# Block sums of the second feed-forward product by accumulating DMAs, its seven products in another order, and small tiles padded

## The chip, the cores and the metric

The kernel runs on 1 core of one Trainium2 chip. The metric is device time in microseconds; 3 runs of the kernel before gave 877.93, 878.17 and 878.65, median 878.17. The profile is of one further execution.

## The reference, cut to what matters

One layer of a streaming encoder on 512 frames of 1024 channels, float32 throughout. Three gated branches (gated linear attention, forgetting attention, attention to 256 memory tokens) are merged and projected, then a feed-forward part follows and a last norm.

```
u = rmsnorm(h) * g_mix
proj = u @ w_in                     # queries, keys, values, gates of three branches
merged = sig(g0)*(o_gla @ w_gla_o) + sig(g1)*(o_fox @ w_fox_o) + sig(g2)*(o_mem @ w_mem_o)
h = h + merged @ w_out
u2 = rmsnorm(h) * g_ffn
h = h + square(relu(u2 @ w_ff1)) @ w_ff2     # 512x1024 @ 1024x4096, then 512x4096 @ 4096x1024
out = rmsnorm(h) * g_final
```

The change concerns the product with `w_ff2` and, by its padding, where some tiles of the branches lie.

## The kernel before

Every large product is done in three TensorE (PE) matmuls: both operands are split into a high part (a cast on ScalarE, ACT) and a low part (a subtraction on VectorE, DVE), and high by high, low by high and high by low are added up in PSUM (`mm3`, lines 118 to 121). Weights come in blocks of 128x1024, 512 KB each, loaded on the SP queue. `split_w` and `split` (lines 111, 112, 171, 172) split them. The hi and lo buffers are three deep (pool `wp`); in the last stage every fourth block uses a buffer of its own, one deep (`bhi`, `blo`, in `split_b`).

The last stage runs over four quarters q of the 4096 hidden channels. A quarter first makes eight 128x512 tiles of the hidden layer, transposed: 24 matmuls with a block of `w_ff1` each, then `act_evac` squares and splits them. Two such tiles make a pair p; of its four 128x256 parts a11, a21 (first tile) and a12, a22 (second) seven forms are kept, in the slots of tiles `ch` and `cl` (high and low): slot 0 as soon as the first tile is there, slots 1 and 2 with the second (a 128x512 split from `sq`), slots 3 to 6 from four differences `ss` (line 888) and a 128x1024 split of them, which is the last to be done.

Then `second(q)` multiplies by the quarter of `w_ff2`, in Strassen's manner (Winograd's form): seven products of half-size blocks in place of eight. Product n takes one slot of the activations and one block of weights. The weights of a quarter are eight tiles `raw`: blocks 11, 12, 22, 21 (stored with the signs that the method needs), each for i = 0 and 1 (pairs 0, 1 and pairs 2, 3). `factor(n, i)` makes the block that product n needs: plain for 1, 2 and 3, and otherwise by adding another block in place on VectorE (`add`, line 906). 5 is block 11 plus 12, 6 is that plus 22, 4 is that plus 21, and 7 is block 12 plus 22. So block 11 is added to three times, each time after the split before has read it. Each step of a product (one i) is 12 matmuls: two row blocks t, two pairs, three matmuls each. The products 1 and 5 stay in PSUM (pool `pa`, tag `a`) over all quarters; 6 and 7 are summed in `R6` and `R7`; 4, 3 and 2 are added to the residual `hN` as they come (`C(i, j, t)` is a 128x512 half of one row block). In the last quarter `evac` combines everything and calls `finish` for each half row: sum of squares on ScalarE, multiplication by the final gain, and behind the second half the row's rsqrt (`ms` on VectorE, `rr` on GpSimd, the POOL engine), two scalings and two stores. The very last product takes both steps i together (`end`).

The order of TensorE is the order in which the program is written. All other engines and the SP queue are ordered by a scheduler when the program is built, so a moved line can move instructions there too. POOL does the merge's additions in the branch stage; between the last of them and the final rsqrts it has only the four rsqrts of the middle norm.

The tiles lie in SBUF pool by pool. A pool on the right side of SBUF holds `acc` and the split branch outputs `ogh`, `ogl` and `omh`, `oml`. They are streamed through TensorE as the moving operand by `branch` (lines 119 to 121 again). In the kernel as built they start 480 bytes past a multiple of 512; `Pm`, `ph` and `pl` of the memory attention start 224 bytes past one; the other large tiles, such as `uhi`, `ofh`, `mh`, `ch`, start 32 past one.

Of the kernel before, what the change touches and what calls it, by code (L numbers as in the profile page):

```python
# [9 lines left out]
F32 = mybir.dt.float32  # L10
# [7 lines left out]
P = 128  # L18
# [14 lines left out]
def chunk_list():  # L33

    L = []
    L += [("T", "w_mem_kv", P * j) for j in range(4)]
    L += [("N", "w_mem_kv", 2 * j, 512) for j in range(4)]
    L += [("G",)]
    L += [("T", "w_in", OFF["fq"]), ("T", "w_in", OFF["fk"])]
    L += [("N", "w_in", 2 * j, OFF["fv"]) for j in range(4)]  # L40
    for j in range(1, 4):
        L += [("T", "w_in", OFF["fq"] + P * j), ("T", "w_in", OFF["fk"] + P * j)]
    for n, c in (("gk", 2), ("gq", 2)):
        L += [("T", "w_in", OFF[n] + P * j) for j in range(c)]
    L += [("N", "w_in", 2 * j, OFF["gv"]) for j in range(4)]
    for n, c in (("gg", 4), ("mq", 4)):
        L += [("T", "w_in", OFF[n] + P * j) for j in range(c)]
    for g, o in (("gate_fox", "w_fox_o"), ("gate_mem", "w_mem_o"), ("gate_gla", "w_gla_o")):
        for j in range(KT):
            L.append(("T", "w_in", OFF[g] + P * j))  # L50
            if j % 2 == 0:
                L.append(("O", o, j // 2))
    for c in range(2):
        L += [("N", "w_out", 2 * j, 512 * c) for j in range(4)]
    for q in range(4):
        L += [("T", "w_ff1", P * (8 * q + j)) for j in range(8)]
        L += [("B", q, i, b) for b in ("11", "12", "22", "21") for i in range(2)]
    return L


# [1 line left out]
def hybrid_block(ctx, tc, chunks, wst, xT, memT, xN, cols, gffn, gfin, wup, cst, out):  # L62
# [6 lines left out]
    def nm(s):  # L69
        uid[0] += 1  # L70
        return f"{s}_{uid[0]}"
# [7 lines left out]
    def pool(name, side=None, bufs=1):  # L79
        return tc.tile_pool(name=name, bufs=bufs, side=side, reuse_waits="tile")  # L80
# [17 lines left out]
    ident, ones, tri, tri64 = (cst_s[:, i * P:(i + 1) * P] for i in range(4))  # L98
    mhalf = cst_s[:, 6 * P:6 * P + 8]
    gmix, gmem, ghead = cols_s[:, 0:8], cols_s[:, 8:16], cols_s[:, 16:20]  # L100

    def load_w(key, eng=None):
        i = index[key]
# [426 lines left out]


    mst = ExitStack()
    mp = mst.enter_context(pool("merge", side="right"))
    acc = [mp.tile([P, S], F32, name=f"acc{j}") for j in range(KT)]

# [37 lines left out]
    with pool("mematt") as ap:  # L573
# [9 lines left out]
        def mem_scores(h):  # L583
            qh, ql = st["q", h]
            mx = ap.tile([P, NT], F32, tag="mx", name=nm("mx"), bufs=2)
            rs = ap.tile([P, NT], F32, tag="rs", name=nm("rs"), bufs=2)
            ri = ap.tile([P, NT], F32, tag="ri", name=nm("ri"), bufs=2)
            Pm = st["p", h] = ap.tile([P, NT, M], F32, tag="Pm", name=nm("Pm"), bufs=2)
            for g in range(2):
                ps = at_([P, 2, M])  # L590
# [42 lines left out]
    with pool("gla") as lp:  # L633
# [13 lines left out]
        def decays(j):  # L647
# [2 lines left out]
                nc.tensor.matmul(pb[:, t * P:(t + 1) * P], la[:, t, j * P:(j + 1) * P], tri64, start=True, stop=True)  # L650
            ep = lp.tile([P, S], F32, tag="ep", name=nm("ep"))
            en = lp.tile([P, S], F32, tag="en", name=nm("en"))
            bl = lp.tile([P, NC, 1], F32, tag="bl", name=nm("bl"))
            dec = lp.tile([P, NC], F32, tag="dec", name=nm("dec"))
            ek = lp.tile([P, NC, 64], F32, tag="ek", name=nm("ek"))
            pb3 = pb.rearrange("p (c t) -> p c t", c=NC)
            nc.vector.tensor_copy(bl, pb3[:, :, 63:64])
# [102 lines left out]

    hp = ctx.enter_context(pool("h"))
    hN = [hp.tile([P, D], F32, name=f"h{t}") for t in range(NT)]
    hss = hp.tile([P, LINE], F32, name="hss")[:, :2 * NT].rearrange("p (t c) -> p t c", c=2)
    gf = hp.tile([P, D], F32, tag="gf", name="gf")
    nc.sync.dma_start(gf, gffn)

# [86 lines left out]
    with pool("ff") as yp:  # L853
# [8 lines left out]
        def split_b(raw):  # L862
            split_n[0] += 1
            own = split_n[0] % 4 == 0
            hi, lo = ((yp if own else wp).tile([P, 1024], F32R, tag=g, name=nm(g), bufs=1 if own else 3)
                      for g in (("bhi", "blo") if own else ("hi", "lo")))
            split(hi, lo, raw)
            return [t.rearrange("p (k c) -> p k c", k=2) for t in (hi, lo)]
# [36 lines left out]
        def add(to, x, op=ALU.add):  # L905
            nc.vector.tensor_tensor(to, to, x, op=op)  # L906

        def evac(q, n, t, ps):
# [24 lines left out]
            if n == 3:  # L933
                add(C(0, 1, t), ps)
                if last:
                    finish(t, 1, 0)
            if n == 2:
                add(C(0, 0, t), ps)
                if last:
                    finish(t, 0, 1)  # L940

        def second(q):
            raw = {(b, i): yp.tile([P, 1024], F32, tag=f"b{b}{i}", name=nm("raw")) for b in ("11", "12", "22", "21")
                   for i in range(2)}
            for (b, i), t in raw.items():
                nc.sync.dma_start(t, wst[index["B", q, i, b]])

            def factor(n, i):

                b11, b12, b22, b21 = (raw[b, i] for b in ("11", "12", "22", "21"))  # L950
                to, x = {1: (b11, None), 5: (b11, b12), 6: (b11, b22), 7: (b12, b22), 4: (b11, b21), 3: (b22, None),
                         2: (b21, None)}[n]
                if x is not None:
                    add(to, x)
                return split_b(to)

            for n, slot in ((1, 0), (5, 3), (6, 4), (7, 5), (4, 2), (3, 6), (2, 1)):
                keep = n in (1, 5)
                if not keep:
                    ps = [mmt() for _ in range(2)]  # L960
                else:
                    ps = held.setdefault(n, [at_() for _ in range(2)] if q == 0 else None)
                end = q == NQ - 1 and n == 2
                steps = [[0, 1]] if end else [[0], [1]]
                for js in steps:
                    w = {i: factor(n, i) for i in js}
# [107 lines left out]
```

## Time and profile before

| | |
|---|---|
| median of 3 runs | 878.17 us (877.93 to 878.65) |
| profiled execution | 879.23 us, span 877.5 us |
| mean granted TensorE clock | 0.988 |
| ScalarE busy in the span | 405.3 us, 46% |
| DMA | 87.75 MB, mean 100 GB/s |
| last stage, four quarters | from about 532 us to the end |

In lines of the timeline the columns are start, duration (both us), engine, line, operation, tiles written and read, shape, count, and in brackets how long the engine sat idle and what ended that. Matmuls overlap: their duration is longer than the distance of their starts, and the distance is what counts for the time. In lines of waits the columns are the total in us, how often, and the longest. In lines of one tile the three numbers are the shortest, median and longest duration in ns. Names in the profile are those of the program without buffer numbers: `a` and `mm` are PSUM tiles, `raw` a loaded block.

### The profile page before, as it was taken

The numbers are of one execution on the slowest core, as the hardware profiler recorded it, in microseconds if no ns is written. First come the engines' busy times: TensorE is split into PE (matmuls) and PEld (weight loads), VectorE is DVE, ScalarE is ACT, GpSimd is POOL, SyncE is SP. The second block draws the span as 40 slices with busy tenths as digits, with TensorE's granted clock in tenths as the row PEclk, the third lists the DMA queues.
The fourth block names the chain that finished last, engine by engine and source line by source line (L and its number), as shares of the span: only waits on it lengthen the run. The fifth ranks groups of instructions, "written<-read, shape, count | busy, mean of one in ns | idle before, by whom it ended". The sixth has DMA issues, their size and how long they took to land.

```text
span 877.5 us, 10602 instructions
## 1 busy us (share of the span) xinstructions
PE 853.3 (97%) x4081; PEld 700.2 (80%) x4081; DVE 533.0 (61%) x854; ACT 405.3 (46%) x644; POOL 53.8 (6%) x58
## 2 busy tenths in 40 slices
PE   7999999999999999999999999989999999899995
PEld 5778788888888888787888889868888888688874
DVE  5784647656444465665434546676578558665787
ACT  7764747654333332222323524644454355335534
POOL 5100000000000011212122000000000000000001
PEclk9999999999999999999999999999999999899998
DMA  8432322222222222134232506314312420251002
GB/s 315 141 120 97 109 96 75 85 69 73 96 92 76 73 72 73 49 97 168 96 96 96 191 1 240 121 49 168 120 49 97 168 96 25 96 167 49 1 1 96
DMA packets 26466, 87.75 MB, mean 100 GB/s; under 512 B 3216, under 2 KB 4016, under 8 KB 26416
## 3 DMA queue, kind: packets, MB, share of 16 engines
q1 hardware_dynamic: 24624, 83.92, 28.3%
q10 hardware_dynamic: 1792, 3.16, 1.1%
q8 instruction: 32, 0.52, 0.2%
q14 instruction: 18, 0.15, 0.1%
HBM read 84.96 MB, written 2.11 MB: 99 GB/s over the span
## 4 chain that ended last, share of the span: by engine, by line
PE 85%; DVE 10%; ACT 2%; issue 1%; DMA 1%; SPq 0%; POOL 0%; ACTq 0%; DVEq 0%; POOLq 0%
PE mm L119 24%; PE mm L120 24%; PE mm L121 24%; DVE lo L172 2%; PE a L121 2%; DVE raw L906 2%; PE a L120 2%; PE a L119 2%; DVE h L906 1%; DVE cl L172 1%; ACT hi L171 1%; PE a L712 1%; DMA cst_s<-in_cst_dram 1%; PE a L445 1%; DVE blo L172 1%
## 5 line engine op out<-in xcount | busy, mean ns | idle before, releaser
L112 DVE TENSOR_TENSOR wlo<-raw,whi 128x1024 fp32r<-128x1024 f32 x104 | 131.1, 1264 | 142.6 <-ACT whi L111 137.8
L111 ACT CAST whi<-raw 128x1024 fp32r<-128x1024 f32 x104 | 109.3, 1052 | 178.6 <-PE mm L120 133.3
L119 PE MATMUL mm<-uhi,whi 128*128 128x512 f32 x360 | 142.6, 396 | 0.0
L120 PE MATMUL mm<-ulo,whi 128*128 128x512 f32 x360 | 140.9, 391 | 1.3 <-DVE ulo L172 1.3
L121 PE MATMUL mm<-uhi,wlo 128*128 128x512 f32 x360 | 140.6, 390 | 0.0
L119 PE MATMUL mm<-u2h,whi 128*128 128x512 f32 x240 | 93.4, 389 | 0.0
L120 PE MATMUL mm<-u2l,whi 128*128 128x512 f32 x240 | 93.4, 389 | 0.0
L121 PE MATMUL mm<-u2h,wlo 128*128 128x512 f32 x240 | 93.4, 389 | 0.0
L120 PEld LDWEIGHTS mm<-ulo,whi 128*128 128x128 f32 x360 | 67.7, 188 | 15.9 <-DVE ulo L172 2.8
L121 PEld LDWEIGHTS mm<-uhi,wlo 128*128 128x128 f32 x360 | 67.6, 188 | 14.7 <-DVE wlo L112 0.4
L119 PEld LDWEIGHTS mm<-uhi,whi 128*128 128x128 f32 x360 | 67.7, 188 | 13.8 <-issue 0.7
L171 ACT CAST hi<-raw 128x1024 fp32r<-128x1024 f32 x42 | 44.0, 1053 | 70.8 <-PE mm L121 29.4
L172 DVE TENSOR_TENSOR lo<-raw,hi 128x1024 fp32r<-128x1024 f32 x42 | 51.2, 1224 | 38.8 <-ACT hi L171 38.8
L121 PEld LDWEIGHTS mm<-u2h,wlo 128*128 128x128 f32 x240 | 45.0, 188 | 9.4
L120 PEld LDWEIGHTS mm<-u2l,whi 128*128 128x128 f32 x240 | 45.0, 188 | 9.4
L119 PEld LDWEIGHTS mm<-u2h,whi 128*128 128x128 f32 x240 | 45.0, 188 | 9.3
L119 PE MATMUL mm<-hi,ch 128*128 128x512 f32 x120 | 47.7, 398 | 0.6 <-DVE hss L771 0.6
L120 PE MATMUL mm<-lo,ch 128*128 128x512 f32 x120 | 47.4, 395 | 0.0
L121 PE MATMUL mm<-hi,cl 128*128 128x512 f32 x120 | 47.4, 395 | 0.0
L906 DVE TENSOR_TENSOR raw<-raw,raw 128x1024 f32<-128x1024 f32 x32 | 39.0, 1220 | 0.2
L565 POOL TENSOR_TENSOR acc<-acc,th 128x512 f32<-128x512 f32 x16 | 24.0, 1502 | 104.0 <-DVE th L564 104.0
L777 POOL TENSOR_TENSOR rr<-ms,cst_s 128x1 f32<-128x1 f32 x8 | 5.2, 653 | 384.1 <-ACT sq L769 341.1
(317 smaller groups left out, 1645.6 us busy)
## 6 DMA issues: line engine op xcount, KB each, us to landing
raw<-in_wst_dram SPq DMA_DIRECT2D x144, 512.0 KB, 3.3
xr<-in_xT_dram SPq DMA_DIRECT2D x4, 512.0 KB, 8.1
nFb<-dF ACTq DMA_DIRECT2D x8, 256.0 KB, 3.3
h<-in_xN_dram SPq DMA_DIRECT2D x4, 512.0 KB, 7.9
memr<-in_memT_dram SPq DMA_DIRECT2D x4, 256.0 KB, 5.8
out_dram<-h ACTq DMA_DIRECT2D x4, 256.0 KB, 2.5
out_dram<-h SPq DMA_DIRECT2D x4, 256.0 KB, 2.2
raw<-in_wst_dram SPq DMA_DIRECT2D x4, 128.0 KB, 5.8
```

Source lines behind the costliest of these rows:

```text
L111: nc.scalar.copy(hi, raw)
L112: nc.vector.tensor_tensor(lo, raw, f(hi), op=ALU.subtract)
L119: nc.tensor.matmul(ps, lh, rh, start=start, stop=False)
L120: nc.tensor.matmul(ps, lh, rl, start=False, stop=False)
L121: nc.tensor.matmul(ps, ll, rh, start=False, stop=stop)
L171: nc.scalar.copy(hi, src)
L172: return nc.vector.tensor_tensor(lo, src, f(hi), op=ALU.subtract).ins
L445: nc.tensor.matmul(ps[:, :w], q, K[e][:, 1, :w], start=False, stop=True)
L565: nc.gpsimd.tensor_tensor(acc[j], acc[j], th, op=ALU.add)
L712: nc.tensor.matmul(ps[:, t, :], kk[:, sl], qq[:, sl], start=True, stop=True)
L777: nc.gpsimd.tensor_tensor(r, ms, mhalf[:, :1], op=ALU.pow)
L906: nc.vector.tensor_tensor(to, to, x, op=op)
```

## The change

Three edits:

1. The products come in the order 1, 2, 5, 6, 7, 4, 3 where it was 1, 5, 6, 7, 4, 3, 2. The blocks are loaded in the order 11, 21, 12, 22 where it was 11, 12, 22, 21. The last product of all is 3 where it was 2, and the second half of rows 0 and 1 to be finished is the one that 3 completes.
2. `factor` no longer adds two SBUF tiles on VectorE (32 instructions of 128x1024 in all). It issues a DMA on the POOL queue that reads the other block from memory again and adds it into the `raw` tile on its way (32 DMAs of 512 KB).
3. `edge` shifts the tiles of the right side by 448 bytes, `stat_pad` is put ahead of `Pm`, and `bl` and `dec` take 512 bytes each. All large tiles named above start 32 bytes past a multiple of 512 then.

```
-        L += [("B", q, i, b) for b in ("11", "12", "22", "21") for i in range(2)]
+        L += [("B", q, i, b) for b in ("11", "21", "12", "22") for i in range(2)]
...
+    def small(pool_, n, tag, name=None, bufs=1):
+        return pool_.tile([P, LINE], F32, tag=tag, name=name or nm(tag), bufs=bufs)[:, :n]
...
+    edge = mst.enter_context(pool("edge", side="right"))
+    edge.tile([P, 112], F32, name="edge_pad")
     mp = mst.enter_context(pool("merge", side="right"))
...
+            if h == 0:
+                ap.tile([P, LINE - 48], F32, name="stat_pad")
             Pm = st["p", h] = ap.tile([P, NT, M], F32, tag="Pm", name=nm("Pm"), bufs=2)
...
-            bl = lp.tile([P, NC, 1], F32, tag="bl", name=nm("bl"))
-            dec = lp.tile([P, NC], F32, tag="dec", name=nm("dec"))
+            bl = small(lp, NC, "bl").rearrange("p (c o) -> p c o", o=1)
+            dec = small(lp, NC, "dec")
...
             if n == 3:
                 add(C(0, 1, t), ps)
                 if last:
-                    finish(t, 1, 0)
+                    finish(t, 1, 1)
             if n == 2:
                 add(C(0, 0, t), ps)
                 if last:
-                    finish(t, 0, 1)
+                    finish(t, 0, 0)
...
-                b11, b12, b22, b21 = (raw[b, i] for b in ("11", "12", "22", "21"))
-                to, x = {1: (b11, None), 5: (b11, b12), 6: (b11, b22), 7: (b12, b22), 4: (b11, b21), 3: (b22, None),
-                         2: (b21, None)}[n]
+                to, x = {1: ("11", None), 5: ("11", "12"), 6: ("11", "22"), 7: ("12", "22"), 4: ("11", "21"), 3: ("22", None),
+                         2: ("21", None)}[n]
                 if x is not None:
-                    add(to, x)
-                return split_b(to)
-            for n, slot in ((1, 0), (5, 3), (6, 4), (7, 5), (4, 2), (3, 6), (2, 1)):
+                    nc.gpsimd.dma_start(raw[to, i], wst[index["B", q, i, x]], accum_op=ALU.add)
+                return split_b(raw[to, i])
+            for n, slot in ((1, 0), (2, 1), (5, 3), (6, 4), (7, 5), (4, 2), (3, 6)):
...
-                end = q == NQ - 1 and n == 2
+                end = q == NQ - 1 and n == 3
```

What that does to VectorE's row in the third quarter, around the last pair of activations (`sq_5931` and `sq_5969`, its differences `ss_5974`). `raw_5981` and `raw_5982` are block 11 for i = 0 and 1, `lo_6031` is its split for product 5, `lo_6067` that for 6. Before:

```order
L172 TENSOR_TENSOR lo_6031<-raw_5981,hi_6030 128x1024
L906 TENSOR_TENSOR raw_5982<-raw_5982,raw_5986 128x1024
L888 TENSOR_TENSOR ss_5974<-sq_5931,sq_5969 128x256
L172 TENSOR_TENSOR cl_5935<-sq_5969,ch_5934 128x512
L906 TENSOR_TENSOR raw_5981<-raw_5981,raw_5985 128x1024
L888 TENSOR_TENSOR ss_5974<-sq_5931,ss_5974 128x256
L888 TENSOR_TENSOR ss_5974<-sq_5969,ss_5974 128x256
L172 TENSOR_TENSOR lo_6067<-raw_5981,hi_6066 128x1024
L172 TENSOR_TENSOR lo_6084<-raw_5982,hi_6083 128x1024
L906 TENSOR_TENSOR raw_5981<-raw_5981,raw_5987 128x1024
L172 TENSOR_TENSOR cl_5935<-ss_5974,ch_5934 128x1024
```

Now, where the pair is `sq_5937`, `sq_5975` and `ss_5980`, block 11 is `raw_5987` and `raw_5988`, and `raw_5989` is block 21 for i = 0:

```order
L176 TENSOR_TENSOR lo_6038<-raw_5989,hi_6037 128x1024
L896 TENSOR_TENSOR ss_5980<-sq_5937,sq_5975 128x256
L896 TENSOR_TENSOR ss_5980<-sq_5937,ss_5980 128x256
L176 TENSOR_TENSOR cl_5941<-sq_5975,ch_5940 128x512
L896 TENSOR_TENSOR ss_5980<-sq_5975,ss_5980 128x256
L176 TENSOR_TENSOR lo_6073<-raw_5987,hi_6072 128x1024
L176 TENSOR_TENSOR cl_5941<-ss_5980,ch_5940 128x1024
L176 TENSOR_TENSOR lo_6090<-raw_5988,hi_6089 128x1024
```

The sums have left the row. The split for product 2 (`lo_6038`) stands at the front, and of the splits of summed blocks only `lo_6073`, for product 5 and i = 0, is still ahead of the last `cl`.

POOL's row between the middle norm and the last stage. Before, the last rsqrts of the middle norm are followed by those of the end:

```order
L777 TENSOR_TENSOR rr_4315<-ms_4314,cst_s 128x1
L777 TENSOR_TENSOR rr_4391<-ms_4390,cst_s 128x1
L777 TENSOR_TENSOR rr_6794<-ms_6793,cst_s 128x1
L777 TENSOR_TENSOR rr_6812<-ms_6811,cst_s 128x1
L777 TENSOR_TENSOR rr_6890<-ms_6889,cst_s 128x1
```

Now the DMAs stand between; in the first quarter `raw_4803` and `raw_4804` are block 12, `raw_4799` and `raw_4800` block 11:

```order
L785 TENSOR_TENSOR rr_4320<-ms_4319,cst_s 128x1
L785 TENSOR_TENSOR rr_4396<-ms_4395,cst_s 128x1
L961 DMA raw_4803<-in_wst_dram 128x1024
L961 DMA raw_4804<-in_wst_dram 128x1024
L961 DMA raw_4799<-in_wst_dram 128x1024
L961 DMA raw_4800<-in_wst_dram 128x1024
```

In each quarter the two sums for product 7 come first, then the pairs for 5, 6 and 4, which write block 11 again and again.

The end of VectorE's row. Before, `h_3609` and `h_3610` are row blocks 0 and 1, `mm_6863` and `mm_6864` the results of product 2, the last one:

```order
L906 TENSOR_TENSOR h_3609<-h_3609,mm_6863 128x512
L771 TENSOR_SCALAR hss<-hss 128x1
L894 TENSOR_TENSOR h_3609<-h_3609,gl 128x512
L771 TENSOR_SCALAR hss<-hss 128x1
L894 TENSOR_TENSOR h_3610<-h_3610,gl 128x512
L899 TENSOR_SCALAR h_3611<-h_3611,rr_6794 128x512
L899 TENSOR_SCALAR h_3612<-h_3612,rr_6812 128x512
L906 TENSOR_TENSOR h_3610<-h_3610,mm_6864 128x512
```

Now, `h_3614` to `h_3617` are the four row blocks, `mm_6869` and `mm_6870` the results of product 3, the last one, and `mm_6810` one of product 4:

```order
L914 TENSOR_TENSOR h_3614<-h_3614,mm_6869 128x512
L779 TENSOR_SCALAR hss_3618<-hss_3618 128x1
L902 TENSOR_TENSOR h_3616<-h_3616,gl 128x512
L914 TENSOR_TENSOR h_3617<-h_3617,mm_6810 128x512
L779 TENSOR_SCALAR hss_3618<-hss_3618 128x1
L902 TENSOR_TENSOR h_3617<-h_3617,gl 128x512
L902 TENSOR_TENSOR h_3616<-h_3616,gl 128x512
L784 TENSOR_SCALAR ms_6843<-hss_3618 128x1
L914 TENSOR_TENSOR h_3615<-h_3615,mm_6870 128x512
L902 TENSOR_TENSOR h_3617<-h_3617,gl 128x512
L784 TENSOR_SCALAR ms_6861<-hss_3618 128x1
L902 TENSOR_TENSOR h_3614<-h_3614,gl 128x512
```

The last product's results now meet the finishing of row blocks 2 and 3, which stood ahead of them before, and the first of its two additions stands in front of one of product 4's.

More of the change, by code (lines that the diff above doesn't have):

```diff
@@ L762, in hybrid_block @@
     hN = [hp.tile([P, D], F32, name=f"h{t}") for t in range(NT)]
-    hss = hp.tile([P, LINE], F32, name="hss")[:, :2 * NT].rearrange("p (t c) -> p t c", c=2)
+    hss = small(hp, 2 * NT, "hss").rearrange("p (t c) -> p t c", c=2)
     gf = hp.tile([P, D], F32, tag="gf", name="gf")
@@ L939, in evac @@
                 if last:
-                    finish(t, 0, 1)
+                    finish(t, 0, 0)
         def second(q):
-            raw = {(b, i): yp.tile([P, 1024], F32, tag=f"b{b}{i}", name=nm("raw")) for b in ("11", "12", "22", "21")
+            raw = {(b, i): yp.tile([P, 1024], F32, tag=f"b{b}{i}", name=nm("raw")) for b in ("11", "21", "12", "22")
                    for i in range(2)}
```

## The prediction

> **What bounds the kernel now.** I read the top of the page first.
>
> ```profile
> span 877.5 us, 10602 instructions
> ...
> PE 853.3 (97%) x4081; PEld 700.2 (80%) x4081; DVE 533.0 (61%) x854; ACT 405.3 (46%) x644; POOL 53.8 (6%) x58
> ```
>
> TensorE (PE) is busy nearly throughout, and VectorE (DVE) is not the bound. An edit that frees VectorE can therefore pay only where TensorE waits. How fast TensorE goes when nothing waits is in its timeline just ahead of the third quarter's second product.
>
> ```profile
> 738.05 0.39 PE L119 MATMUL mm<-u2h,whi 128*128 128x512 f32 x1
> ...
> 740.77 0.39 PE L119 MATMUL a<-hi,ch 128*128 128x512 f32 x1
> ```
>
> Twelve matmuls start in these 2.72 us, one per 0.2267 us. A product of the second feed-forward product is two steps (i = 0, 1) of 12 matmuls, so a step is 2.72 us and a product 5.44 us. Next I asked for the waits between 560 and 870 us, and followed them in the timeline.
>
> ```profile
> PE a L121 <- DVE cl L172: 5.7, 4, 2.0
> PE a L119 <- ACT ch L171: 1.2, 2, 0.6
> PE mm L119 <- DVE hss L771: 0.6, 1, 0.6
> ```
>
> ```profile
> 748.03 0.39 PE L121 MATMUL a<-bhi,cl 128*128 128x512 f32 x1
> 749.03 0.50 PE L119 MATMUL a<-bhi,ch 128*128 128x512 f32 x1 [0.61 <-ACT ch L171]
> 749.37 0.39 PE L120 MATMUL a<-blo,ch 128*128 128x512 f32 x1
> 751.79 0.80 PE L121 MATMUL a<-bhi,cl 128*128 128x512 f32 x1 [2.03 <-DVE cl L172]
> ...
> 757.50 0.58 PE L119 MATMUL mm<-hi,ch 128*128 128x512 f32 x1
> 757.92 0.40 PE L120 MATMUL mm<-lo,ch 128*128 128x512 f32 x1
> ```
>
> In the third quarter 17 matmuls take 9.89 us from 748.03 to 757.92, where 3.85 would do: 6.0 us lost. The starts around the two waits lie 1.00 and 2.42 us apart, 3.0 more than normal. The other 3.0 is that the matmuls behind come every 0.42 us. The table by stage shows the granted clock below 1 in the first and third quarter, the two with such a stretch (the columns behind the engines are the clock, the share of the DMA engines and GB/s).
>
> ```profile
> 532.00:614.00 82.00, 79.36 (x367) 65.98 (x366) 55.89 (x67) 39.79 (x52) 0.00 (x0) 0.98 0.43 151
> ...
> 695.00:778.00 83.00, 80.36 (x341) 65.69 (x340) 53.39 (x66) 37.86 (x48) 0.00 (x0) 0.96 0.28 92
> ```
>
> The other three quarters and the end, first and last row of each disturbed stretch (13, 2, 2 and 2 matmuls):
>
> ```profile
> 579.49 0.39 PE L121 MATMUL a<-bhi,cl 128*128 128x512 f32 x1
> 587.25 0.39 PE L119 MATMUL mm<-hi,ch 128*128 128x512 f32 x1
> 666.39 0.39 PE L120 MATMUL a<-lo,ch 128*128 128x512 f32 x1
> 667.31 0.39 PE L119 MATMUL a<-hi,ch 128*128 128x512 f32 x1
> 836.13 0.39 PE L120 MATMUL a<-lo,ch 128*128 128x512 f32 x1
> 838.24 0.40 PE L119 MATMUL a<-hi,ch 128*128 128x512 f32 x1
> 861.18 0.39 PE L121 MATMUL mm<-hi,cl 128*128 128x512 f32 x1
> 862.45 0.40 PE L120 MATMUL mm<-lo,ch 128*128 128x512 f32 x1
> ```
>
> At 0.2267 us each they lose 7.76 - 2.95 = 4.8, 0.92 - 0.45 = 0.5, 2.11 - 0.45 = 1.7 and 1.27 - 0.45 = 0.8 us. The four quarters lose 13.0 us in all.
>
> What TensorE waits for is cl, the low half of the last activation pair's sums, needed by the product that stands second in a quarter. VectorE's timeline says why it is late.
>
> ```profile
> 747.11 2.36 DVE L172 TENSOR_TENSOR lo<-raw,hi 128x1024 fp32r<-128x1024 f32 x2 [0.38 <-ACT hi L171]
> 749.39 1.22 DVE L906 TENSOR_TENSOR raw<-raw,raw 128x1024 f32<-128x1024 f32 x1
> 750.52 1.22 DVE L172 TENSOR_TENSOR cl<-ss,ch 128x1024 fp32r<-128x1024 f32 x1
> ```
>
> Sums of weight blocks (raw<-raw,raw) and the splits that need them stand ahead of cl in its queue.
>
> **The change, part by part.**
>
> *Sums off VectorE, plain product second.*
>
> ```profile
> L906 DVE TENSOR_TENSOR raw<-raw,raw 128x1024 f32<-128x1024 f32 x32 | 39.0, 1220 | 0.2
> ```
>
> This removes 39.0 us of VectorE work, 8 sums per quarter. By itself it is worth nothing, since VectorE is not the bound. Its worth is at the four waits. In the new order rows no sum stands ahead of the last cl, and only one split of a summed block does. Product 2 (no sum, slot 1) now runs where product 5 ran, so the last cl (slots 3 to 6) is needed 5.44 us later. The worst stretch without a start was 2.42 us. Both edits push the same way with more than is needed, so I take all four waits as gone, with the slow clock that followed two of them: -13.0 us.
>
> Is product 2 itself late? Its slot 1 comes with a plain 128x512 split, which in the new VectorE order stands ahead of the summed split. It needs block 21, which the load order now puts second. No.
>
> *What is new: 32 accumulating DMAs of 512 KB, issued on the POOL queue.* Behind a waiting one on POOL stand only the next ones and, at the end, four tiny rsqrt steps. The split of the summed block waits for it on ScalarE and VectorE, and behind that split stand cl, other splits and evacuations. No row shows an accumulating DMA, so the room that it has is worked out first.
>
> ```profile
> 842.61 1.05 ACT L171 CAST hi<-raw 128x1024 fp32r<-128x1024 f32 x1 [1.73 <-PE mm L121]
> 845.33 1.05 ACT L171 CAST bhi<-raw 128x1024 fp32r<-128x1024 f32 x1 [1.67 <-PE mm L121]
> ```
>
> ```profile
> 843.70 1.23 DVE L172 TENSOR_TENSOR lo<-raw,hi 128x1024 fp32r<-128x1024 f32 x1 [1.55 <-ACT hi L171]
> ```
>
> ```profile
> 853.25 0.39 PE L119 MATMUL mm<-bhi,ch 128*128 128x512 f32 x1
> ```
>
> A block's cast starts when a buffer comes free, 853.25 - 845.33 = 7.92 us ahead of its first matmul, and a split takes 843.70 + 1.23 - 842.61 = 2.32 us. The narrowest place is product 6 right behind 5: block 11 may be summed again only after split (5,i), done 5.60 us ahead of that step, and split (6,i) must start 2.32 us ahead of a step 5.44 us later. Room: 5.60 + 5.44 - 2.32 = 8.7 us from release to landing. The sum for 5 is released by the split for 1, over 8 us before it is wanted; the sum for 4 has 5.44 us more because 7 lies between; the sum for 7 writes block 12, which nobody reads before, and goes first.
>
> ```profile
> raw<-in_wst_dram SPq DMA_DIRECT2D x144, 512.0 KB, 3.3
> xr<-in_xT_dram SPq DMA_DIRECT2D x4, 512.0 KB, 8.1
> ```
>
> A plain load of the same bytes lands after 3.3 us, or after 8.1 us queued in the crowded start. An accumulate moves the block from memory and reads the old one as well. Its bounds are 3.3 (one load) and 16.2 us (two crowded ones); I take 6.6, two undisturbed loads, since the DMA engines are 28 to 43% busy here, near the undisturbed row. It fits the 8.7 us with 2.1 to spare, so it costs nothing; without that cover each microsecond over 8.7 costs one per quarter.
>
> The Trainium skill (Collectives: The Full Stack, "The bandwidth ceiling") says that the add in the DMA is free and that the two source reads on one ring halve the rate. By that an accumulate would take up to twice the plain row, 6.6 us, and by the plain row alone 3.3; the sum is the same by either, only the room left over differs, and no run so far shows which.
>
> *The end.* The 0.8 us wait at 862 us was for evacuations ahead of the last product's buffers; now those buffers are product 7's, emptied a product earlier: -0.8. After the last matmul:
>
> ```profile
> 867.45 0.39 PE L121 MATMUL mm<-bhi,cl 128*128 128x512 f32 x1
> ```
>
> ```profile
> 852.50 2.50 DVE L906 TENSOR_TENSOR h<-h,sq 128x512 f32<-128x512 f32 x4
> ...
> 871.27 0.21 DVE L776 TENSOR_SCALAR ms<-hss 128x1 f32<-128x1 f32 x1
> ```
>
> ```profile
> 872.93 0.72 ACT L897 ACTIVATE h<-h,rr 128x512 f32<-128x512 f32 x1 [0.42 <-ACT h L897]
> ```
>
> Before, the last rsqrt input (ms) starts 3.4 us behind the last matmul's end. In the new order VectorE stands still until half of product 3 is done, 2.7 us ahead of the end, then has nine passes of some 0.6 us (the x4 row) and eight short ones, about 1.5 us together by my estimate, up to its last ms: 4.2 us behind the end, 0.8 later. But the other row block is finished by then, and the final scaling is one deep instead of two (0.72 us of ScalarE, the last row). Net +0.1, bounds -0.7 and +1.5.
>
> *Padding.* It moves omh, oml, ogh, ogl and ph, pl from 480 or 224 bytes past a multiple of 512 to 32, where ofh lies already.
>
> ```profile
> L119 PE MATMUL mm<-ofh,whi x32: 388/389/476, 234.3 to 318.0; 128*128 128x512 f32 x32
> ```
>
> ```profile
> L119 PE MATMUL mm<-ogh,whi x32: 394/394/394, 419.0 to 478.9; 128*128 128x512 f32 x32
> ```
>
> ```profile
> L119 PE MATMUL a<-ph,mvh x8: 394/394/394, 258.5 to 313.2; 128*128 128x512 f32 x8
> ```
>
> Matmuls that stream the shifted tiles take 394 ns, every one; the others 388 or 389. If the address is why, 192 + 24 matmuls save 5.5 ns each: -1.2 us; bounds -1.3 and 0. The other padded tiles are read by a few short operations: 0.
>
> *Sum.* -13.0 - 0.8 + 0.1 - 1.2 = -14.9 us. The profiled execution took 879.23 us (span 877.5 and 1.7 around it), so 864.3 for it. It lies 1.06 above the median 878.17 of the runs, which gives **863.3 us**.
>
> **Rivals.**
>
> *A late sum (slower).* If an accumulate takes L over 8.7 us, TensorE waits L - 8.7 at product 6 in each quarter; steps behind it have slipped too and do not pay again. With 2.42 us between starts the clock fell, which cost 3.0 us in the third quarter and 4.8 - 3.0 = 1.8 in the first; with 2.1 us for two matmuls (836 us) it did not fall. Taking 2.4 for that, the gain of 14.9 is used up at L = 8.7 + 3.7 - 2.4 = 10.0 if the clock falls, at 12.4 if not. At L = 13.2 (twice my value) it costs 4 x (4.5 + 2.4) = 27.6 us: 891 us. For it: no row shows such a transfer, and sums and loads share the engines. Against: the spare 2.1 us. 0.14.
>
> The Trainium skill (TensorE: Matmul & The Clock Gate, Part 1) has the clock fall after an idle window of about 3.4 us. Here it fell after 2.42, so the trace decides; by the page alone the slow matmuls (4.8 us in two quarters) would not be the waits' doing, would stay, and 868 us would come out.
>
> *A sum slightly late.* L of 9 to 10.5 costs 0.3 to 1.8 per quarter without the clock, 1 to 7 us: 864 to 871. 0.15.
>
> *The waits stay.* If ScalarE's order rather than the sums makes cl late, or the wait moves to the summed split ahead of it, only padding and end are gained: about 877. Against: the busy VectorE rows above. 0.05.
>
> **How the numbers follow.** The forecast (0.66) has its own range, 862 to 866, from the bounds of end and padding. With the slightly late sum and part of the third rival, the range for 8 in 10 is 862 to 876. A measurement of this kernel can tell about 0.2% (1.8 us) from no change. Faster 0.81 (forecast and slightly late sum), same 0.05, slower 0.14.
>
> **What would show it.** Right: no wait on cl in TensorE's list; granted clock 1.00 in all four quarters; TensorE's steps 2.72 us apart from product 1 to 3; accumulating DMAs landing under 8.7 us; matmuls on ogh at 389 ns. Wrong: TensorE or the cast waiting for a POOL DMA at product 6, four times, and a slow clock behind it.

## The result, and the profile after

The changed kernel takes 865.02 us (median of 4 runs, 863.63 to 865.56) against 878.17 (4 runs): a ratio of 0.9847, with a 95% interval of 0.983 to 0.9864, so 13.2 us less. Forecast were 863.3 us and a range of 862 to 876. The profiled execution took 863.63 us, 1.4 below the median.

The top of the page after. VectorE lost 36 us of busy time and GpSimd gained 28; TensorE has 10 us less of "busy" for the same 4081 matmuls.

```profile
span 861.9 us, 10680 instructions
...
PE 843.2 (98%) x4081; PEld 696.3 (81%) x4081; DVE 497.2 (58%) x822; ACT 406.6 (47%) x644; POOL 82.0 (10%) x90
```

The table by stage for the first and the third quarter (moved back by 3.35 us, since the last stage starts that much earlier). TensorE is busy for all of both stretches and the granted clock is 1.00, where it was 0.98 and 0.96.

```profile
528.65:610.65 82.00, 82.00 (x389) 68.98 (x388) 47.76 (x60) 40.99 (x53) 9.76 (x11) 1.00 0.80 225
691.65:774.65 83.00, 83.00 (x368) 68.76 (x367) 47.74 (x60) 40.90 (x51) 7.88 (x9) 1.00 0.59 155
```

In the third quarter each row below is the first matmul of a product, in the order 1, 2, 5, 6, 7, 4, 3. They stand 5.44 us apart, every one: the pitch of 0.2267 us is kept from end to end, and TensorE's list of waits is empty from 528 us on. Before, product 5 began at 749.03 behind a wait, and another wait followed inside it.

```profile
730.72 0.39 PE L123 MATMUL a<-hi,ch 128*128 128x512 f32 x1
736.16 0.39 PE L123 MATMUL mm<-hi,ch 128*128 128x512 f32 x1
741.60 0.39 PE L123 MATMUL a<-hi,ch 128*128 128x512 f32 x1
747.04 0.39 PE L123 MATMUL mm<-hi,ch 128*128 128x512 f32 x1
752.48 0.39 PE L123 MATMUL mm<-hi,ch 128*128 128x512 f32 x1
757.92 0.39 PE L123 MATMUL mm<-hi,ch 128*128 128x512 f32 x1
763.36 0.39 PE L123 MATMUL mm<-hi,ch 128*128 128x512 f32 x1
```

The accumulating DMAs. The first two rows are from the list of DMA issues (median from issue to landing), the third is GpSimd issuing the first sum for product 6, the last is ScalarE's cast of that sum, released by the landing.

```profile
raw<-in_wst_dram SPq DMA_DIRECT2D x144, 512.0 KB, 3.3
raw<-in_wst_dram POOLq DMA_DIRECT2D x32, 512.0 KB, 5.3
```

```profile
736.25 0.88 POOL L961 DMA_DIRECT2D raw<-in_wst_dram  x1 [7.51 <-DVE lo L176]
```

```profile
741.32 1.05 ACT L175 CAST hi<-raw 128x1024 fp32r<-128x1024 f32 x1 [3.90 <-DMA raw<-in_wst_dram]
```

From 736.25 to 741.32 are 5.1 us, and product 6 starts at 747.04, 5.7 us behind the start of the cast. The cast follows the landing at once, yet TensorE does not wait for it.

Where the time went is read at three places of TensorE's row. Each pair of rows below is the first matmul of the first large projection, the first one of the second feed-forward product, and the last one of all; before, then after.

```profile
40.65 0.39 PE L119 MATMUL mm<-uhi,whi 128*128 128x512 f32 x1
570.88 0.39 PE L119 MATMUL a<-hi,ch 128*128 128x512 f32 x1
```

```profile
38.85 0.39 PE L123 MATMUL mm<-uhi,whi 128*128 128x512 f32 x1
567.52 0.39 PE L123 MATMUL a<-hi,ch 128*128 128x512 f32 x1
850.18 0.39 PE L125 MATMUL mm<-bhi,cl 128*128 128x512 f32 x1
```

- Up to the first row: 40.65 and 38.85, 1.80 less.
- From there to the second: 530.23 and 528.67, 1.56 less.
- From there to the end of the last matmul (867.84 and 850.57): 296.96 and 283.05, 13.9 less.
- The tail, to the end of the span (877.45 and 861.85): 9.6 and 11.3, 1.7 more.

The first of these can't be put down to the change. Over the 14 profiled executions of this study, one of each kernel, that row lies between 38.85 and 42.26 us, with the instructions up to there the same; both ends of that range are kernels with the padding and the DMAs. The granted clock of the first 30 us differs as well (0.94 before, 1.00 after):

```profile
0.00:30.00 30.00, 24.80 (x141) 19.10 (x142) 19.19 (x28) 22.14 (x45) 11.23 (x16) 0.94 0.75 270
```

```profile
0.00:30.00 30.00, 24.59 (x148) 19.21 (x149) 17.92 (x28) 23.09 (x48) 11.96 (x16) 1.00 0.78 285
```

The pieces behind the start repeat within some 0.1 us from kernel to kernel where an edit doesn't touch them (the product is 283.04 us in five of them). Whole runs scatter far more: 17 runs of the kernel before on one chip took 873.38 to 881.08 us, more than the 3.4 us of the start, and what else moves there is not shown. The experiments are therefore read by their pieces, each from one profiled execution, and the medians only confirm them.

### The profile page after: what moved, and what is told of

Read it like the earlier page. It is cut to its first block, busy times and chain, and to the rows that moved or that the text cites. A ratio compares the mean times of both kernels' runs of the same rounds, so it can differ in the third digit from the quotient of the medians.

```text
span 861.9 us, 10680 instructions
## 1 busy us (share of the span) xinstructions
PE 843.2 (98%) x4081; PEld 696.3 (81%) x4081; DVE 497.2 (58%) x822; ACT 406.6 (47%) x644; POOL 82.0 (10%) x90
## 4 chain that ended last, share of the span: by engine, by line
PE 91%; DVE 4%; ACT 2%; issue 1%; DMA 1%; SPq 0%; POOL 0%; ACTq 0%; DVEq 0%; POOLq 0%
PE mm L123 25%; PE mm L124 25%; PE mm L125 24%; PE a L123 3%; PE a L125 3%; PE a L124 3%; DVE h L914 1%; PE a L720 1%; DMA raw<-in_wst_dram 1%; PE a L449 1%; PE a L737 1%; PE a L480 1%; PE a L479 1%; PE a L731 1%; PE a L447 1%
## 5 line engine op out<-in xcount | busy, mean ns | idle before, releaser
L961 POOL DMA_DIRECT2D raw<-in_wst_dram x32 | 28.1, 879 | 277.1 <-DVE lo L176 201.5
L176 DVE TENSOR_TENSOR cl<-ss,ch 128x1024 fp32r<-128x1024 f32 x16 | 19.6, 1225 | 13.4 <-ACT ch L175 13.4
```

Of the source, the lines that this page charges most:

```text
L176: return nc.vector.tensor_tensor(lo, src, f(hi), op=ALU.subtract).ins
L961: nc.gpsimd.dma_start(raw[to, i], wst[index["B", q, i, x]], accum_op=ALU.add)
```

## The experiments

Theory: each of the two edits alone moves the last cl by more than its lateness, so either removes the waits; the DMA costs nothing as long as a sum lands within some 8.7 us of its release; the tail is longer because of the order. Rivals: both edits are needed; the DMA is late somewhere; the tail is the DMA's doing.

All twelve in one table. "Product" is from the first matmul on ch to the end of the last matmul of all, "tail" from there to the end of the span, both of the profiled execution. The ratio is to the kernel before, timed on the same chip.

| kernel | median us | ratio (95%) | product | tail |
|---|---|---|---|---|
| before | 878.17 | | 296.96 | 9.6 |
| changed kernel | 865.02 | 0.9847 (0.983 to 0.9864) | 283.04 | 11.3 |
| e1_order_only | 868.52 | 0.9899 (0.9876 to 0.9921) | 283.04 | 12.7 |
| e2_dma_only | 866.33 | 0.9871 (0.9846 to 0.9897) | 284.09 | 9.8 |
| e3_pads_only | 874.77 | 0.9972 (0.9949 to 0.9995) | 296.90 | 9.6 |
| e4_no_pads | 867.23 | 0.9883 (0.9858 to 0.9908) | 283.04 | 11.3 |
| e5_sum_twice | 930.99 | 1.059 (1.0562 to 1.0619) | 352.38 | 9.7 |
| e6_gain_on_pool | 865.58 | 0.9856 (0.9841 to 0.987) | 283.33 | 11.1 |
| e7_sum_later | 909.9 | 1.0383 (1.0344 to 1.0423) | 328.86 | 11.1 |
| e7b_sum_later_still | 986.72 | 1.1268 (1.1231 to 1.1305) | 405.99 | 8.2 |
| e8_sums_on_pool | 866.25 | 0.9876 (0.9857 to 0.9895) | 283.04 | 12.5 |
| e9_last_quarter_old_order | 864.63 | 0.9856 (0.9835 to 0.9876) | 283.92 | 9.8 |
| e10_gain_fused | 864.07 | 0.9834 (0.9805 to 0.9862) | 283.04 | 10.4 |
| e11_best | 864.25 | 0.9838 (0.9813 to 0.9864) | 284.26 | 8.6 |

**The order alone.** The kernel before with the new orders of loads and products, and with the last quarter's `end` and `finish` to match:

```
-            for n, slot in ((1, 0), (5, 3), (6, 4), (7, 5), (4, 2), (3, 6), (2, 1)):
+            for n, slot in ((1, 0), (2, 1), (5, 3), (6, 4), (7, 5), (4, 2), (3, 6)):
```

> The products and blocks in the new order (1, 2, 5, 6, 7, 4, 3), the sums of blocks still on VectorE, no padding. My theory (either of the two edits moves the last cl by more than the worst 2.42 us gap): no wait on cl in the last stage, granted clock 1.00 in all four quarters, the last matmul's end 13 to 14 us earlier against the start of the last stage than before, and the tail behind the last matmul about as long as in the changed kernel (11.3 us), since the order makes it; time 878.2 - 13.8 + 1.7 = 866 us. Rival (both edits are needed, the sums on VectorE still delay the splits): waits of 0.5 to 2 us stay in two or more quarters, 869 to 876 us. On the tail: if the 32 accumulating DMAs lengthened it, it is 9.7 to 10.5 us here.

The first matmul on ch, the last matmul, and the span with its clock:

```profile
571.11 0.39 PE L119 MATMUL a<-hi,ch 128*128 128x512 f32 x1
...
853.76 0.39 PE L121 MATMUL mm<-bhi,cl 128*128 128x512 f32 x1
```

```profile
core 0: 866.8 us, clock 0.991
```

853.76 + 0.39 - 571.11 = 283.04 us, what the changed kernel takes, with no wait of TensorE at all. The order by itself removes everything. The 39 us of sums on VectorE cost nothing there; in the tail, which was expected to be 11.3 as in the changed kernel, they go with 1.4 us more (12.7). The median, 868.52, is 2.5 us above what was expected, and that tail is 1.4 of it.

**The DMAs alone.**

```
-                if x is not None:
-                    add(to, x)
+                if x is not None:
+                    nc.gpsimd.dma_start(raw[to, i], wst[index["B", q, i, x]], accum_op=ALU.add)
```

> The accumulating DMAs in place of the sums on VectorE, the products in the old order (1, 5, 6, 7, 4, 3, 2), no padding. My theory (either edit alone is enough): 865 to 867 us, no wait on cl. Rival (the order does the work, and the DMA is slower than the sum that it replaces): with 5 second, the split for product 6 still stands ahead of the last cl on ScalarE and VectorE, and now waits for a transfer of 5.4 us in place of a sum of 1.2 us, so cl comes some 4 us later than before; TensorE's gap of 2.4 us in the worst quarter grows to 4 to 6 us in every quarter, the clock falls behind it, and the time is 885 to 905 us.

Its list of TensorE's waits from 532 us on has one row, the wait near the end that was there before:

```profile
PE mm L119 <- DVE hss L771: 0.5, 1, 0.5
```

```profile
848.57 0.39 PE L121 MATMUL mm<-hi,cl 128*128 128x512 f32 x1
849.48 0.47 PE L119 MATMUL mm<-hi,ch 128*128 128x512 f32 x1 [0.53 <-DVE hss L771]
```

The product takes 284.09 us: 1.05 more than with the new order, of which about 0.8 is that wait and 0.3 stands at 825 us, in the last quarter, where the split for 6 is ahead of cl. So the theory holds (either edit is enough), and the rival that this kernel would be slower than before falls: in the third quarter the last cl stood ahead of the split for 6. Here the tail is 9.8 us, with the DMAs: they are not what lengthens it. Product and tail together take 293.9 us, where the changed kernel takes 294.3: with the DMAs in place, the new order gains 1.05 us in the product and loses 1.5 in the tail.

**The padding alone, and all but the padding.** e3 is the kernel before with `edge`, `stat_pad` and the two tiles of `small`; e4 is the changed kernel without them.

```
+    edge = mst.enter_context(pool("edge", side="right"))
+    edge.tile([P, 112], F32, name="edge_pad")
...
+                ap.tile([P, LINE - 48], F32, name="stat_pad")
```

> The kernel before with the padding alone. My theory (216 matmuls on the shifted tiles go from 394 to 389 ns and nothing else moves): 1.2 us less, 877.0 us, ogh, ogl, omh, oml, ph and pl at 388 or 389 ns. Rival (the 1.7 us that the changed kernel gains between 230 and 480 us on matmuls are all the padding's, and short operations gain too): 1.7 to 2.0 us less, 876.3 us. Second rival (the offset is not the reason): the matmuls stay at 394 ns, 878.2 us.

> The changed kernel without the padding. If the parts add up: 865.0 + 1.2 = 866.2 us by my theory, 865.0 + 1.7 = 866.7 by the rival that the padding is worth more; 865.0 if the offset is not the reason. The last stage is as in the changed kernel: no waits of TensorE, tail of 11.3 us.

The matmuls on ogh in e3, and where the first matmul on ofh and on ch stand in the changed kernel (the latter is above):

```profile
L123 PE MATMUL mm<-ogh,whi x32: 389/389/390, 417.4 to 476.5; 128*128 128x512 f32 x32
```

```profile
L123 PE MATMUL mm<-ofh,whi x32: 389/389/476, 232.6 to 316.1; 128*128 128x512 f32 x32
```

From the first matmul on ofh to the first on ch are 336.6 us before (570.88 - 234.27) and in e4, 334.9 in the changed kernel (567.52 - 232.59) and in e3: the padding is worth 1.7 us, whether the rest of the change is there or not. That is the rival's figure (1.7 to 2.0), not the 1.2 of my theory. The distances between the starts of matmuls on ogh fell from 0.2333 to 0.2267 us. Matched one by one, the kernel before against e3, the 216 matmuls on shifted tiles give 1.28 us and the others of that stretch 0.44. Of the others it is mostly single ones on uhi, which did not shift; they started 0.231 to 0.236 us apart and now 0.227. Why the padding reaches them is not shown. The medians of e3 and e4 (3.4 us less than before, 2.2 more than the changed kernel) contain the starts of their executions and can't tell 1.2 from 1.7.

**A sum that takes two transfers.**

```
                 if x is not None:
                     nc.gpsimd.dma_start(raw[to, i], wst[index["B", q, i, x]], accum_op=ALU.add)
+                    nc.gpsimd.dma_start(raw[to, i], wst[index["B", q, i, x]], accum_op=ALU.add)
```

> The changed kernel with each accumulating DMA issued twice, one behind the other, so that a sum takes two transfers (the other block is added two times, so products 5, 6, 7 and 4 are of other numbers). In the changed kernel an undisturbed one takes 5.1 to 6.2 us from issue to landing and 0.3 us more from the split that releases it, so a sum takes 10.5 to 12 us here. My step (room of 8.7 us at product 6, each microsecond over it costs one per quarter): TensorE waits some 2 to 3.5 us at product 6 in each quarter, the clock falls behind the longer ones, 865.0 + 8 to 24 = 873 to 889 us. Rival (the room is larger than I worked out, since steps run ahead): under 870 us. Rival (the later sums pay as well, for 6 and 4): over 889 us.

GpSimd's waits from 560 us on, and TensorE ahead of product 6 in the first quarter:

```profile
POOL raw L962 <- DMA raw<-in_wst_dram: 126.5, 30, 8.2
```

```profile
590.22 0.63 PE L125 MATMUL a<-hi,cl 128*128 128x512 f32 x1
596.09 0.80 PE L123 MATMUL mm<-hi,ch 128*128 128x512 f32 x1 [5.24 <-ACT hi L175]
```

930.99 us, far above the range of my step; of the rivals it is the third, later sums pay as well (product 4 loses 6 to 7 us in each quarter). The second DMA of a pair waits in GpSimd's queue for the first one's landing, 126.5 us in all, and the sums behind it stand in the same queue. I had priced the transfer and not the queue. So this run doesn't measure the room; it shows that a sum that blocks GpSimd's queue is dear.

**A sum released later.** A multiplication by 1.0 in place on GpSimd delays the issue without a wait for a landing; e7b has two of them.

```
                 if x is not None:
+                    nc.gpsimd.tensor_scalar(raw[to, i], raw[to, i], 1.0, None, op0=ALU.mult)
                     nc.gpsimd.dma_start(raw[to, i], wst[index["B", q, i, x]], accum_op=ALU.add)
```

> The changed kernel with one multiplication of the raw tile by 1.0 on GpSimd (in place, 128x1024) between the split that releases a sum and its accumulating DMA, so that a sum is later by the time of that multiplication (about 1.5 to 3 us, from 1.38 us of GpSimd for 128x512 with two inputs), and GpSimd's queue is not held up by a transfer. Release to landing was 5.4 us in the median of the undisturbed sums; here 7 to 8.5. My step (room of 8.7 us at product 6): no wait of TensorE, 865 us, and 283.0 us from the first matmul on ch to the last one's end, as in the changed kernel. Rival (the room is smaller, since casts stand ready right behind a landing already): waits of 0.5 to 3 us per quarter, 867 to 880 us.

> The same with two multiplications: release to landing of 8.5 to 11.5 us. My step (each microsecond over 8.7 costs one per quarter, and a slow clock behind gaps of 2.4 us and more): 0 to 2.8 us per quarter and up to 2.4 for the clock, 866 to 886 us, with TensorE's gaps at product 6. Rival (the room is larger): 865 us. Rival (later sums pay again): gaps at product 4 as well, over 886 us.

The first sum for product 6 in the first quarter of e7: the split that releases it, GpSimd (the multiplications of both steps' sums, then the two issues), the cast, and TensorE.

```profile
572.99 1.22 DVE L176 TENSOR_TENSOR lo<-raw,hi 128x1024 fp32r<-128x1024 f32 x1
```

```profile
574.31 6.42 POOL L961 TENSOR_SCALAR raw<-raw 128x1024 f32<-128x1024 f32 x2 [3.81 <-DVE lo L176]
580.69 1.81 POOL L962 DMA_DIRECT2D raw<-in_wst_dram  x2
```

```profile
586.05 1.04 ACT L175 CAST hi<-raw 128x1024 fp32r<-128x1024 f32 x1 [9.90 <-DMA raw<-in_wst_dram]
```

```profile
585.07 0.39 PE L125 MATMUL a<-hi,cl 128*128 128x512 f32 x1
587.15 0.50 PE L123 MATMUL mm<-hi,ch 128*128 128x512 f32 x1 [1.69 <-ACT hi L175]
588.41 0.50 PE L124 MATMUL mm<-lo,ch 128*128 128x512 f32 x1 [0.76 <-DVE lo L176]
588.75 0.40 PE L125 MATMUL mm<-hi,cl 128*128 128x512 f32 x1
```

This is the room, measured. The split ends at 574.21 and the cast starts at 586.05, right behind the landing: 11.8 us. TensorE loses (587.15 - 585.07) + (588.41 - 587.15) - 2 x 0.2267 = 2.9 us. A sum may therefore take 8.9 us without any loss; worked out ahead were 8.7. The other quarters give 8.8, 9.0 and 8.8 in the same way. In the changed kernel the eight sums for product 6 take 5.0 to 6.2 us from issue and are issued some 0.3 us behind their release, so over 2 us are spare.

Both expectations for e7 missed (865, and 867 to 880 for the rival). The delay was larger than I expected: a multiplication of 128x1024 takes 2.8 to 3.7 us, and two stand ahead of two issues. The price was larger still: 909.9 us, 45.8 in the product, 11.5 per quarter. The first step of product 6 loses 3.0, 5.6, 4.5 and 5.7 us in the four quarters, 2.9 to 3.5 of it at the late sum and the rest in slow matmuls right behind it. Its second step loses 3.0 in all, and product 4 loses 23.8, half of everything. The likely reason is GpSimd's queue, in which the multiplications and issues for 4 stand behind those for 6. e7b, at 986.72, goes further the same way: product 4 loses 9 to 24 us in each quarter, as the last of its rivals had it.

**The tail: work taken off VectorE.** In e6 GpSimd does the gain of the half rows that are finished first, in e8 the six additions of product 6's results that read SBUF alone:

```
-            nc.vector.tensor_tensor(hN[t][:, cs], hN[t][:, cs], gl[:, cs], op=ALU.mult)
+            eng = nc.gpsimd if n == 0 else nc.vector
+            eng.tensor_tensor(hN[t][:, cs], hN[t][:, cs], gl[:, cs], op=ALU.mult)
```

```
-                add(C(1, 0, t), E)
-                add(C(1, 1, t), G)
-                add(C(0, 1, t), G)
+                for to, x in ((C(1, 1, t), G), (C(1, 0, t), E), (C(0, 1, t), G)):
+                    nc.gpsimd.tensor_tensor(to, to, x, op=ALU.add)
```

> The changed kernel with the multiplication by the final gain of the half rows that are finished first (4 of 8, 128x512 each) on GpSimd in place of VectorE. If the tail's extra 1.7 us come from VectorE's row, which runs without a break from 847 us to the last ms at 855.3 us, taking 4 x 0.60 us out of it makes ms come up to 2.4 us earlier: 862.6 to 864.0 us, tail of 9 to 10.3 us. Rival (the tail hangs on POOL and on the output DMAs): no change, or slower by the 1.5 us that POOL takes for such a multiplication ahead of a rsqrt, 865 to 866.5 us.

> The changed kernel with the six additions of product 6's results in the last quarter that read SBUF alone (E and G into the rows of h, 128x512 each) on GpSimd in place of VectorE. Theory: the tail is 1.7 us longer than before because VectorE's row is behind by then, product 6 with its twelve passes standing 5.44 us nearer to the end. Taking 6 x 0.62 = 3.7 us out of the row some 8 us ahead of the end lets it catch up: tail of 9.6 to 10.2 us in place of 11.3, 863.4 to 864.0 us. Rival (the tail is made by the order of the last steps themselves, as the kernel with the gain on GpSimd suggests, whose tail stayed at 11.1): 11.0 to 11.4 us, 865 us.

Tails of 11.1 and 12.5 us: next to nothing gained in e6, 1.2 lost in e8, more than even its rival had (11.0 to 11.4). In e8, GpSimd's additions and what VectorE did beside them:

```profile
840.99 8.10 POOL L931 TENSOR_TENSOR h<-h,sq 128x512 f32<-128x512 f32 x4
```

```profile
837.94 1.94 DVE L176 TENSOR_TENSOR lo<-raw,hi 128x1024 fp32r<-128x1024 f32 x1
...
844.47 5.77 DVE L914 TENSOR_TENSOR h<-h,R 128x512 f32<-128x512 f32 x4
```

An addition takes GpSimd 2.0 us in the mean (VectorE 0.6), VectorE's split beside it 1.94 us in place of 1.22, and four of its additions 5.77 us in place of 2.50. So work moved to GpSimd slowed VectorE by about 4.0 us (0.7 and 3.3), more than the six additions of 0.6 that it took off. The Trainium skill (SBUF — State Buffer, "Who interferes with whom") has VectorE and GpSimd exclude each other on one shared pair of ports; these rows agree. As a test of the tail e8 is spoilt by that. e6 is no clean test either: one multiplication of VectorE beside GpSimd's takes 1.11 us in place of 0.69, and VectorE comes to the last product's results only 1.9 us ahead of the last matmul's end, 2.5 in the changed kernel.

**The tail: the order of the last quarter.**

```
+            order = ((1, 0), (2, 1), (5, 3), (6, 4), (7, 5), (4, 2), (3, 6))
+            if q == NQ - 1:
+                order = (order[0],) + order[2:] + (order[1],)
```

> The changed kernel with the products of the last quarter alone in the old order (1, 5, 6, 7, 4, 3, 2), the first three quarters in the new one. Theory: the tail returns to the 9.6 to 9.8 us of before and of the kernel with the DMAs alone, and the last quarter has the losses that the latter had there (0.26 us at 825 us and 0.77 us at 849 us), so 284.1 us from the first matmul on ch to the last one's end: 0.5 us less than the changed kernel in all, 864.5 us. Rival (the tail is the DMAs' or the padding's): 11.3 us.

```profile
855.04 0.21 DVE L784 TENSOR_SCALAR ms<-hss 128x1 f32<-128x1 f32 x1
```

With its last matmul ending at 851.61, the last ms is 3.4 us behind, as before, and the tail 9.8 us. The product takes 283.92 us. Together that is 0.65 less than the changed kernel; 0.5 were expected. So the order of the last quarter makes the tail.

**The tail: fewer passes of VectorE, and both.** e10 takes the gain of the half that is finished second into its scaling; e11 is that with the order of e9.

```
-            nc.vector.tensor_tensor(hN[t][:, cs], hN[t][:, cs], gl[:, cs], op=ALU.mult)
-            if n == 1:
+            if n == 0:
+                nc.vector.tensor_tensor(hN[t][:, cs], hN[t][:, cs], gl[:, cs], op=ALU.mult)
+            else:
...
+                nc.vector.scalar_tensor_tensor(hN[t][:, cs], hN[t][:, cs], r, gl[:, cs], op0=ALU.mult, op1=ALU.mult)
```

> The changed kernel with the final gain of the half row that is finished second taken into its scaling (one pass of VectorE, row times rsqrt times gain, in place of two), the other half being scaled on ScalarE: four passes of 0.60 us less in VectorE's row at the end, and nothing on GpSimd. Theory (VectorE's row, without a break up to the last ms, makes the tail): the last ms starts 1.2 to 2.4 us earlier against the last matmul, tail of 9.0 to 10.1 us in place of 11.3, 863 to 864 us. Rival (the tail hangs on ScalarE's squares, POOL's rsqrts and the stores): tail of 11.0 to 11.4 us, 865 us.

> Both together on the changed kernel: the last quarter in the old order, and the gain taken into the scaling. If the two add up: 283.9 us from the first matmul on ch to the last one's end (as with the old order alone), tail of 8.3 to 9.2 us, together 1.2 to 2.1 us less than the changed kernel: 863 to 864 us. Rival (behind the last product the chain addition, square, rsqrt, scaling, store is as long as before whatever VectorE's row holds): tail of 9.5 to 9.8 us, 864.5 us.

The last ms of e10, whose last matmul ends at 852.76:

```profile
856.11 0.21 DVE L784 TENSOR_SCALAR ms<-hss 128x1 f32<-128x1 f32 x1
```

It lies 3.4 us behind that end, where the changed kernel has 4.8: 1.4 earlier for four passes of 0.6. The tail is 10.4, only 0.9 shorter, just outside what was expected; its last scaling starts 5.7 us ahead of the span's end (5.2 in the changed kernel), so half a microsecond went to the stores. In e11 the tail is 8.6 us and the product 284.26: 292.9 together against 294.3, the best of all. Its median, 864.25, is 0.8 below the changed kernel's, within the scatter of the starts; that it is faster is shown by the pieces alone.

## Why the prediction was right, and where not

- **The four waits and the slow clock behind two of them: right.** -13.0 and, for the wait at the end, -0.8 were forecast, -13.9 measured. Each edit is enough by itself, as the step said: the order fully (e1), the DMAs but for 0.3 us in the last quarter (e2). With the waits the slow matmuls went too. The Trainium skill (TensorE: Matmul & The Clock Gate, Part 1) wants an idle window of about 3.4 us before matmuls go slow; the rival drawn from it, slow matmuls that stay, is refuted, since all four quarters run at 1.00.
- **The accumulating DMA at no cost: right.** 6.6 us were taken for a sum, and 5.3 is the median. The six with no other sum or block load under way take 5.1 to 5.2. Of all 32, 25 take 5.0 to 6.2 and seven 7.1 to 11.9. Six of the seven are sums for product 7, which go first and have time; the seventh (7.1) is for product 4. TensorE waits for none of them. The room was 8.8 to 9.0 where 8.7 was worked out. The Trainium skill (Collectives: The Full Stack, "The bandwidth ceiling") has an add free and the second source halve the rate. From issue to landing the rows give 5.1 against 3.3 us, a factor of 1.5. But the 3.3 are of loads on the SP queue, and no run has a plain load on GpSimd's, so what the second source costs is not shown.
- **The padding: right for the tiles that it priced, too small in all.** -1.2 with a bound of -1.3, measured -1.7. The 216 matmuls on shifted tiles give 1.28, as the step said. The other 0.4 is on matmuls of tiles that did not shift, which the step put at nothing.
- **The tail: wrong.** +0.1 with a bound of +1.5, measured +1.7. VectorE's and ScalarE's rows of the changed kernel, the last matmul ending at 850.57:

```profile
845.63 2.50 DVE L914 TENSOR_TENSOR h<-h,R 128x512 f32<-128x512 f32 x4
848.04 1.29 DVE L914 TENSOR_TENSOR h<-h,mm 128x512 f32<-128x512 f32 x2
...
854.32 0.69 DVE L902 TENSOR_TENSOR h<-h,gl 128x512 f32<-128x512 f32 x1
854.92 0.49 DVE L907 TENSOR_SCALAR h<-h,rr 128x512 f32<-128x512 f32 x1
855.32 0.22 DVE L784 TENSOR_SCALAR ms<-hss 128x1 f32<-128x1 f32 x1
```

```profile
855.51 0.72 ACT L905 ACTIVATE h<-h,rr 128x512 f32<-128x512 f32 x1 [0.42 <-POOL rr L785]
...
856.65 0.72 ACT L905 ACTIVATE h<-h,rr 128x512 f32<-128x512 f32 x1 [0.42 <-POOL rr L785]
```

  Three sizes were off. Ten passes and two scalings stood ahead of the last ms, not nine passes: it came 4.75 us behind the last matmul, not 4.2 (3.43 before). The other row block was not finished by then: the scaling is still two deep (between the two rows of ScalarE stands the issue of the first one's store, 0.34 us at 856.26, which doesn't count as busy), and its last one starts 1.33 us behind ms, 0.33 sooner than before, not 0.72. And the stores take longer: 5.2 us from the last scaling's start to the end of the span, 4.5 before (877.45 - 872.93), which the step left out. 0.55 + 0.39 + 0.68 = 1.6, the whole miss. e9 shows that the order of the last quarter is the cause. That it works by the finishing of row blocks 2 and 3 meeting the last product's is read from these rows, and e10 bears it out in part: four passes fewer bring the last ms 1.4 us forward. Why the stores take longer is open.
- **The sum.** By pieces the change is -13.9 - 1.7 + 1.7 = -13.9 us, against -14.9 forecast: 1.6 too little in the tail, 0.5 more than thought from the padding, 0.1 at the waits. It is luck that the padding's surplus hid a third of the tail's miss. The medians differ by 13.15; the other 0.7 is less than the starts scatter.
- **The late sum, the rival on the other side: did not come.** Its condition was right (a room of 8.8 to 9.0), its price too low. By its rule, 2.9 and 2.4 for the clock, 5.3 us per quarter would be lost in e7. The first step of product 6 does lose that, 3.0 to 5.7. But the rule had the steps behind a late one not pay again, and they did: 11.5 us per quarter, most of the rest at product 4.

## What to carry to other kernels

When TensorE waits for an operand, ask first whether another product can stand in that place: here the reordering alone did what moving 39 us of work to the DMA did, to within 1.05 us, and in the product both together did no more than the reordering. Price a slower producer by its room, from the release of its buffer to the first use of its result, and price being late by all the steps that pay, down the queue that it holds up, not by the lateness alone. And a new order moves the end as well: count what the finishing engine has in its row behind the last matmul, down to the stores.

## What was not expected of the hardware

- An accumulating DMA of 512 KB into SBUF, issued on GpSimd, takes 5.1 us from issue to landing with no other block transfer under way, 5.3 in the median of 32; a plain load on the SP queue takes 3.3. Its issue holds GpSimd for 0.88 us.
- Matmuls that stream ogh from 480 or ph from 224 bytes past a multiple of 512 start 0.2333 us apart, from 32 bytes past one 0.2267.
- The clock doesn't fall behind every wait. In e7, the matmuls behind the starts 2.08 and 1.26 us apart, shown above, kept their pitch for over 2 us. Behind the two waits below they came every 0.43 from 604.4 us on, and the granted clock of that stretch was 0.58. In the third quarter starts 2.23 and 1.26 us apart, much like the first pair, had the slow matmuls behind them (from 778.5 us). The Trainium skill (TensorE: Matmul & The Clock Gate, Part 1) lets its window run freely, by which the same gap would count once and not another time; no run here tests that.

```profile
601.90 0.50 PE L123 MATMUL mm<-hi,ch 128*128 128x512 f32 x1 [1.02 <-ACT hi L175]
603.16 0.50 PE L124 MATMUL mm<-lo,ch 128*128 128x512 f32 x1 [0.76 <-DVE lo L176]
...
604.80 0.63 PE L124 MATMUL mm<-lo,ch 128*128 128x512 f32 x1
605.23 0.63 PE L125 MATMUL mm<-hi,cl 128*128 128x512 f32 x1
```

```profile
604.00:607.00 3.00, 3.00 (x9) 1.95 (x7) 1.47 (x2) 0.23 (x1) 0.53 (x1) 0.58 0.93 191
```

- The first 40 us, with the same instructions in all 14 kernels, differ by up to 3.4 us between their profiled executions, more than most edits here are worth.
